# A two-group encoder layer on one core: the second unit's PSUM copies and sum moved ahead of row squares and of the third unit's weights, and the token tiles' transposes moved three steps on

## The chip, the core and the metric

The kernel runs on one core of a Trainium2 chip. A core has engines that run side by side, each with a queue of its own that it works through strictly in order: TensorE (PE in the profile; its weight loads are PEld), VectorE (DVE), ScalarE (ACT), GpSimd (POOL) and SyncE (SP, here used to issue DMAs). An instruction at the head of a queue that waits for another engine holds up all that is queued behind it. Matmuls write into the eight banks of PSUM, and ACT or DVE has to read a bank before other data may be written into it. The metric is the device time of one execution in microseconds; it was 1259.35 us in the median of three runs of the kernel before (1260.97, 1259.35, 1259.35).

## The reference, cut to what matters

One encoder layer is applied to 1024 tokens of a prompt and 256 of a sample, 1280 tokens of 1024 features, with the same weights:

```
h = rms_norm(x, norms[0])
b, c, v = split(h @ conv_w_in, 3)          # 1024 -> 3 x 1024
u = c * v
conv = sum(up[:, j:j + S] * conv_w[j] for j in range(3))
x = x + rms_norm((b * conv) @ conv_w_out, norms[1])
h = rms_norm(x, norms[2])
gate, up = split(h @ ffn_w_in, 2)          # 1024 -> 2 x 2816
x = x + rms_norm((silu(gate) * up) @ ffn_w_out, norms[3])
```

All is float32.

## The kernel before, in words

A float32 product is computed as three matmuls: each operand is split into a high part (a rounded copy, made by ACT) and a low part (what is left, by a DVE subtraction), and high x high, high x low and low x high are added in PSUM. `split`, line 92, does both steps; `make` (line 186) does it for weights, `hi_lo` and `parts` for activations.

The products with the 1024 prompt tokens go by a scheme of seven products of half-size blocks instead of eight. It needs sums and differences of blocks of the activations (the tiles s1 to s4) and of the weights (`make(u, "sums")`, then the pairs t13 and t24). One such product is 12 matmuls of 128x128 by 512 columns (line 213). The sample's 256 tokens are multiplied plainly. A `Block` (line 219) holds one unit, that is, the 128 output features of each of two weight tiles; its products go into the banks x, y and z, and an `Ev` class reads them: `read11`, `read12`, `copy22` and `read21` are ACT copies or DVE products out of bank x between two products that go on accumulating in it, `add11`, `add12` and `add22` are DVE sums that take in bank y or z.

The program has these stages: the first three units of the convolution, called c, v and b (`start`, line 527), the other nine units (loop at line 785), the product with conv_w_out with two norms and transposes back to feature order, by token tiles (loop at line 923), the first FFN product (`ffn_in`), and the second (from line 1553).

Two parts set the order of the work in different ways. `start` and the entry into the FFN stand inside `tc.manual_schedule()`: there each engine's queue has exactly the written order. The loops at lines 785 and 923 stand outside: there a scheduler orders the instructions when the kernel is built, from its own estimate of times, and it may also place instructions of the automatic part between those of `start` that are still to come.

**In `start`, lines 675 to 708.** The second unit (v) has its weights uv, the third (b) ub. TensorE's order is: the product with t24 and s2 into bank x (line 684, below "x6"), t13 with s1 into z (line 689, "z5"), t13 with s3 on top of x (line 690, "x7"), eight small matmuls that spread the norms of the first token chunk over the partitions (`spread(0, 5)`, line 694), t24 with a22 on top of x (line 702, "x4"), and the weights u with s4 on top of z (line 707, "z4"). Then the third unit begins (line 712). x7 may not start before `read12` (line 685) has copied bank x, x4 not before `copy22` (line 692), z4 not before `add22` (line 697) has taken in bank z, and z4 also needs both parts of s4. On ACT, rows of x are squared and summed for the first norm (`next_row`, line 660, which then issues the DMA of a later row from SP's queue into the place that is freed). `norm_of` (line 493) turns the sums into factors with a DVE operation and a power on POOL, and `parts_of_norm` (line 500) makes rq and the high and low parts rh and rl, which `spread` needs.

**In the loop at line 923.** Ten token tiles, in the order 0, 4, 1, 5, 2, 6, 3, 7, then 8 and 9 in the FFN's entry. A tile's product `mm2` (line 847) has eight steps k of six matmuls. After it comes a chain: squares on ACT, factor on DVE and POOL, norm and residual on DVE, squares again, factor again, and the tile ht (line 889). Its eight transposes on TensorE (line 817) are put inside the product of the tile after next, behind `early` of its steps; two copies, one each by ACT and DVE, take them out of PSUM, and `early_sums` (line 910) forms sums from them. The loop's index n counts tiles in this order.

Of the kernel before, what the change touches and what calls it, by code (L numbers as in the profile page):

```python
# [16 lines left out]
KD = D // P  # L17
# [19 lines left out]
def encoder_kernel(ctx: ExitStack, tc: tile.TileContext, xT, x, g0T, gB, cwT, w1, w2, w3, w4, out_p, out_s):  # L37
# [20 lines left out]
    def get(name, shape, dt=F32, kind="b"):  # L58
        if kind == "as":
            kind = "s" if free["s"] else "a"  # L60
        tag = free[kind].pop(0)
        t = mem.tile([P, *shape], dt, tag=tag, name=name)
        held[id(t)] = (t, tag)
        return t

    def put(*tiles):
        for t in tiles:
            tag = held.pop(id(t))[1]
            free[tag[0]].append(tag)
# [19 lines left out]
    def f32(ap):  # L89
        return ap.bitcast(F32)  # L90

    def split(hi, lo, src):
        nc.scalar.activation(hi, src, AF.Copy)
        nc.vector.tensor_tensor(out=lo, in0=src, in1=f32(hi), op=ALU.subtract)

    def sub(out, a, b):
        nc.vector.tensor_tensor(out=out, in0=a, in1=b, op=ALU.subtract)  # L97

    def add(out, a, b):
        return nc.vector.tensor_tensor(out=out, in0=a, in1=b, op=ALU.add)  # L100

    def mul(out, a, b):
        nc.vector.tensor_tensor(out=out, in0=a, in1=b, op=ALU.mult)

    def copy(out, a):
        nc.scalar.activation(out, a, AF.Copy)  # L106
# [3 lines left out]
    def new_ps(name, bank=None):  # L110

        if bank is None:
            bank = turn[0] % 8
            turn[0] += 1
        return ps.tile([P, 512], F32, tag=f"bank{bank}", name=name)
# [9 lines left out]
    def small(n, name, dt=F32):  # L125
        return tmp.tile([P, 4], dt, tag="small", name=name, bufs=8)[:, :n]
# [41 lines left out]
    def uname(u):  # L168
        return "".join(map(str, u))
# [16 lines left out]
    def make(u, what):  # L186

        if u is None:
            return
        rw = raw[u]  # L190
        if what == "sums":
            sub(rw[:, 0], rw[:, 1], rw[:, 0])
            sub(rw[:, 1], rw[:, 2], rw[:, 1])
            sub(rw[:, 2], rw[:, 0], rw[:, 2])
            add(rw[:, 3], rw[:, 3], rw[:, 2])
            return
        blocks = {"g": slice(0, 4, 3), "u": slice(1, 3), "t13": slice(0, 2), "t24": slice(2, 4)}[what]
        t = wb[what, u] = get(f"w{what}{uname(u)}_", [2, 2, 512], F32R)
        split(t[:, 0], t[:, 1], rw[:, blocks])
        sums_made[u] = sums_made.get(u, 0) + what.startswith("t")  # L200
        if sums_made[u] == 2:
            put(raw.pop(u))
# [279 lines left out]
    def load_row(i):  # L482
        sq_rows[i] = get(f"rows{i}", [D], kind="a")
        nc.sync.dma_start(sq_rows[i], x[i])

    def square_row(i):
        t = sq_rows.pop(i)
        nc.scalar.activation(t, t, AF.Square, accum_out=rt[:, i : i + 1])
        put(t)
# [10 lines left out]
    def parts_of_norm(c):  # L500
        t0, n = CH[c]
        i0, m = t0 // P, n // P
        rc = rt[:, i0 : i0 + m]
        mul(rq[:, i0 : i0 + m], rc, rc)
        norms[c] = [small(m, f"r{p}{c}", F32R) for p in "hl"]
        split(*norms[c], rc)

    def spread(c, bank):

        n = CH[c][1]  # L510
        bc = new_ps(f"bc{c}", bank)
        for i in range(n // P):
            for j in range(2):
                nc.tensor.matmul(
                    bc[:, i * P : (i + 1) * P], norms[c][j][:, i : i + 1].to_broadcast([P, P]), ident_r,
                    start=j == 0, stop=j == 1,
                )
        if c < 2:
            nc.scalar.activation(prompt(r2, c), bc, AF.Square)
        else:  # L520
            nc.scalar.activation(samp(r2), by_halves(bc), AF.Square)

    def new_c(name):
        cb[name] = [get(f"{name}{p}", [KH, 512], F32R) for p in "hl"]
        return cb[name]

    def start():
# [85 lines left out]
        def scaled_add(out, src, f0, other, op=ALU.add):  # L613
            for k in range(KH):
                nc.vector.scalar_tensor_tensor(
                    out=out[:, k], in0=src[:, k], scalar=g0k(f0 + k), in1=other[:, k], op0=ALU.mult, op1=op
                )

        def parts(name, src):
            hi, lo = new_c(name)  # L620
            for k in (0, 2):
                copy(hi[:, k : k + 2], src[:, k : k + 2])
            for k in (0, 2):
                sub(lo[:, k : k + 2], src[:, k : k + 2], f32(hi[:, k : k + 2]))


        s1, s2, s3, s4 = (xq[q] for q in ("a21", "a11", "a22", "a12"))
# [14 lines left out]
        ev = EvMul(2, 0)  # L642
        b = Block(uv, ev, banks={q: new_ps(f"{q}v_", n) for q, n in (("x", 0), ("y", 1), ("sg", 2), ("su", 3), ("z", 4))})
# [16 lines left out]
        def next_row(i):  # L660
            square_row(i)
            if i + 2 < NT:
                load_row(i + 2)
# [12 lines left out]
        high3(0)  # L676
        high3(2)
        low3()
        next_row(4)
        parts_of_norm(0)  # L680
        scaled_add(s4, xq["a12"], KH, s2)
        put(s2, s3)
        next_row(5)
        b.run("x", "t24", 0, "s2", False)
        ev.read12(b.bank["x"])
        ev.add11(b.bank["y"], mult=False)
        parts("s4", s4)
        put(s4)
        b.run("z", "t13", 0, "s1", True)
        b.run("x", "t13", 1, "s3", False)  # L690
        b.drop("t13")
        ev.copy22(b.bank["x"])
        make(ub, "g")
        spread(0, 5)
        make(ub, "u")
        make(ub, "sums")
        ev.add22(b.bank["z"])
        next_row(6)
        next_row(7)
        load(SEQ[3])  # L700
# [57 lines left out]
    with tc.manual_schedule():  # L758
        start()
# [25 lines left out]
    for n in range(3, len(SEQ)):  # L785
# [3 lines left out]
        ev = EvC(u[2]) if u[1] == 1 else EvMul(u[1], u[2])  # L789
# [3 lines left out]
        b = Block(u, ev, *follow[:2], final)  # L793
# [23 lines left out]
    def transposes(i, banks=(None, None)):  # L817
        for q in range(2):
            o = new_ps(f"tr{i}_{q}", banks[q])
            for k in range(4):  # L820
                nc.tensor.transpose(
                    o[:, k * P : (k + 1) * P], hts[i][:, (4 * q + k) * P : (4 * q + k + 1) * P], ident
                )
            ov = o.rearrange("p (k t) -> p k t", k=4)
            if i < 8:
                t0 = i % 4 * P
                dst = ar[q, i // 4][:, :, t0 : t0 + P]
                if q:
                    nc.vector.tensor_copy(dst, ov)
                else:  # L830
                    copy(dst, ov)
            else:
                t0 = (i - 8) * P
                copy(hs[0][:, 4 * q : 4 * q + 4, t0 : t0 + P], ov)
                left.append((i, q, ov))
        put(hts.pop(i))
# [10 lines left out]
    def mm2(*tiles, ks=range(KD)):  # L847
        for i in tiles:
            if i not in mx:
                mx[i] = [new_ps(f"mx{i}_{h}", MX_BANKS.get((i, h))) for h in range(2)]  # L850
        for k in ks:
            for i in tiles:
                for j, (w, part) in enumerate(TERMS):
                    for h in range(2):
                        nc.tensor.matmul(  # L855
                            mx[i][h], zs[i][:, part, k], w2t[k][:, w, h * H : (h + 1) * H],
                            start=k == 0 and j == 0, stop=k == KD - 1 and j == 2,
                        )
# [51 lines left out]
    def early_sums(t):  # L910

        a, b, d = (q[:, :, t] for q in (a11, a21, a22))
        split(*(q[:, :, t] for q in cb["a11"]), a)
        add(b, b, d)
        sub(a, a, b)
        add(s3[:, :, t], d, a)
# [6 lines left out]
    for n, i in enumerate(ORDER2[:8]):  # L923
        if n == 0:
            mm2(i, ORDER2[1])
        elif n > 1:
            early = KD - 2 if n < 4 else 1
            mm2(i, ks=range(early))
            transposes(ORDER2[n - 2])
            mm2(i, ks=range(early, KD))  # L930
            if n == 4:
                cb["a11"] = [get(f"a11{p}", [KH, 512], F32R) for p in "hl"]
                s3 = get("s3", [KH, 512])
                early_sums(slice(0, P))
            if n == 6:
                early_sums(slice(P, 2 * P))
        after_mm2(i)
        if n:
            load_z(ORDER2[n + 1])
            load_xt(ORDER2[n + 1])  # L940
        if n == 4:
            load(F0)
            for what in ("g", "u", "sums"):
                make(F0, what)
        if n == 6:
            for what in ("t24", "t13"):
                make(F0, what)
# [691 lines left out]
```

## Time and profile before

| | |
|---|---|
| median of three runs | 1259.35 us |
| the profiled execution, its own time | 1260.64 us |
| its span in the profile | 1258.8 us |
| granted TensorE clock, mean | 0.995 of full speed |
| TensorE busy | 1239.4 us, 98% of the span |
| DVE busy | 834.9 us, 66% |
| ACT busy | 464.2 us, 37% |
| POOL busy | 26.1 us, 2% |

The table is read from the first part of the profile's page and from the run's record. A row of the timeline gives the start and the duration of an instruction (or of a merged run of equal ones, with xcount), its engine, line and operation, what it writes and reads, and in brackets how long the engine had been idle before it and what ended that. Matmuls are pipelined: a row shows 0.39 us for a matmul where the next one starts 0.23 us later. In tile names v and b stand for the second and third unit: xv and zv are banks x and z of the second, xb and zb of the third, wrp__152 are the third unit's raw weights and wrp__611 the fourth's.

### The profile page before, as it was taken

To read this page: it belongs to the slowest core of one execution; us is meant where nothing else is said; L and a number is where in the kernel's file an instruction comes from. 1 tells how busy PE (TensorE), PEld (TensorE's weight loads), DVE (VectorE), ACT (ScalarE), POOL (GpSimd) and SP (SyncE) were. 2 spreads that over 40 slices of the span, in tenths; PEclk is the share of its full clock that TensorE was granted. 3 is DMA by queue.
4 is the path that set the end of the run, shared out by engine and by line. 5 is a ranking of instruction groups with operands and counts; after the bars stand their busy time and mean duration, and the time that the engine had idled before them with its cause. 6 is when DMAs were issued, how large, how long until landed. Compare 5 with 4: busy or idle time off the path is not lost.

```text
span 1258.8 us, 15941 instructions
## 1 busy us (share of the span) xinstructions
PE 1239.4 (98%) x6239; PEld 1053.5 (84%) x6239; DVE 834.9 (66%) x1157; ACT 464.2 (37%) x695; POOL 26.1 (2%) x49
## 2 busy tenths in 40 slices
PE   9899999999999999999999999999999999999997
PEld 7788888888878888888888888888888888888886
DVE  6967855747276697466565764765657479869566
ACT  8633333325143464343343442433434342112011
POOL 0000000000011000000000000000000000000000
PEclk9999999999999999999999999999999999999999
DMA  8313132225954215253453542533526888866894
GB/s 304 110 55 117 68 117 67 81 88 183 318 179 156 101 35 176 92 192 99 136 159 98 171 142 80 184 124 111 192 77 196 282 303 300 272 218 211 287 332 177
DMA packets 186123, 207.37 MB, mean 165 GB/s; under 512 B 8000, under 2 KB 146368, under 8 KB 185024
## 3 DMA queue, kind: packets, MB, share of 16 engines
q1 hardware_dynamic: 185616, 205.83, 48.9%
q8 instruction: 49, 0.80, 0.3%
q10 hardware_dynamic: 432, 0.53, 0.1%
q14 instruction: 26, 0.21, 0.1%
HBM read 134.89 MB, written 71.43 MB: 164 GB/s over the span
## 4 chain that ended last, share of the span: by engine, by line
PE 87%; DVE 5%; DMA 4%; ACT 2%; issue 1%; POOL 1%; SPq 0%; POOLq 0%; DVEq 0%; ACTq 0%
PE xo L1438 12%; PE zo L1438 6%; PE mx L855 5%; PE yo L1438 3%; DMA wrf__3033<-w 1%; PE xf__7466 L213 1%; PE xp__1068 L213 1%; PE xb__651 L213 1%; PE xf__3503 L213 1%; PE xf__4931 L213 1%; PE xf__7645 L213 1%; PE xf__7253 L213 1%; PE xf__7079 L213 1%; PE xf__6866 L213 1%; PE xf__6692 L213 1%
## 5 line engine op out<-in xcount | busy, mean ns | idle before, releaser
L855 PE MATMUL mx<-w2s,zs 128*128 128x512 f32 x480 | 111.1, 391 | 0.0
L855 PEld LDWEIGHTS mx<-w2s,zs 128*128 128x128 f32 x480 | 89.5, 188 | 18.2
L106 ACT ACTIVATE st<-act 128x640 fp32r<-128x640 f32 x77 | 56.8, 737 | 93.6 <-DMA actd<-st 62.7
L97 DVE TENSOR_TENSOR st<-act,st 128x640 fp32r<-128x640 f32 x77 | 63.2, 821 | 21.3 <-ACT st L106 20.8
L100 DVE TENSOR_TENSOR y<-y,xo 128x512 f32<-128x512 f32 x85 | 58.3, 685 | 27.4 <-PE xo L1438 27.1
L1438 PE MATMUL xo<-w4t,us 128*128 128x512 f32 x273 | 68.9, 389 | 0.0
L1438 PEld LDWEIGHTS xo<-w4t,us 128*128 128x128 f32 x273 | 51.3, 188 | 10.6
L1438 PE MATMUL xo<-w4t,ut 128*128 128x512 f32 x222 | 55.5, 389 | 0.0
L106 ACT ACTIVATE w4t<-w4r 128x1024 fp32r<-128x1024 f32 (+1 forms) x23 | 23.5, 1023 | 72.8 <-DVE w4r L97 59.7
L1438 PEld LDWEIGHTS xo<-w4t,ut 128*128 128x128 f32 x222 | 41.7, 188 | 8.7
L100 DVE TENSOR_TENSOR y<-y,zo 128x512 f32<-128x512 f32 x45 | 30.8, 685 | 17.3 <-PE zo L1438 16.9
L1438 PE MATMUL xo<-w4b,ut 128*128 128x512 f32 x165 | 41.6, 390 | 0.0
L1438 PE MATMUL zo<-w4t,ut 128*128 128x512 f32 x165 | 41.5, 389 | 0.0
L1438 PE MATMUL zo<-w4b,ut 128*128 128x512 f32 x165 | 41.5, 389 | 0.0
L1470 ACT ACTIVATE junk<-y 128x1024 f32<-128x1024 f32 (+1 forms) x12 | 11.0, 919 | 73.7 <-DVE y L100 72.3
L1438 PEld LDWEIGHTS xo<-w4b,ut 128*128 128x128 f32 x165 | 31.0, 188 | 6.6
L1438 PEld LDWEIGHTS zo<-w4t,ut 128*128 128x128 f32 x165 | 31.0, 188 | 6.5
L1438 PEld LDWEIGHTS zo<-w4b,ut 128*128 128x128 f32 x165 | 31.0, 188 | 6.4
L430 DVE SCALAR_TENSOR_TENSOR row<-u,cw,row 128x1024 f32<-128x1024 f32 (+1 forms) x32 | 27.7, 880 | 3.7 <-ACT row L428 3.5
L1438 PE MATMUL yo<-w4b,us 128*128 128x512 f32 x114 | 28.9, 389 | 0.0
L106 ACT ACTIVATE w4b<-w4r 128x512 fp32r<-128x512 f32 (+1 forms) x22 | 18.1, 838 | 28.9 <-PE zo L1438 12.5
L97 DVE TENSOR_TENSOR w4t<-w4r,w4t 128x1024 fp32r<-128x1024 f32 (+1 forms) x23 | 26.9, 1174 | 0.8 <-ACT w4t L106 0.8
(2115 smaller groups left out, 3350.9 us busy)
## 6 DMA issues: line engine op xcount, KB each, us to landing
actd<-st SPq DMA_DIRECT2D x154, 320.0 KB, 2.8
ut<-actd SPq DMA_DIRECT2D x20, 1024.0 KB, 6.3
us<-actd SPq DMA_DIRECT2D x62, 256.0 KB, 5.1
ut<-actd SPq DMA_DIRECT2D x16, 768.0 KB, 7.9
zd<-zst SPq DMA_DIRECT2D x32, 320.0 KB, 3.0
zs<-zd SPq DMA_DIRECT2D x8, 1024.0 KB, 6.6
w4r<-w SPq DMA_DIRECT2D x11, 512.0 KB, 4.3
w4r<-w SPq DMA_DIRECT2D x22, 256.0 KB, 5.0
```

Source lines behind the costliest of these rows:

```text
L97: nc.vector.tensor_tensor(out=out, in0=a, in1=b, op=ALU.subtract)
L100: return nc.vector.tensor_tensor(out=out, in0=a, in1=b, op=ALU.add)
L106: nc.scalar.activation(out, a, AF.Copy)
L213: nc.tensor.matmul(out[:, :n], stat(w, k), mov(part, k), start=first and k == 0 and j == 0, stop=last and k == KH - 1 and j == 2, skip_gro ...
L430: nc.vector.scalar_tensor_tensor(out=out, in0=src, scalar=cw[:, j, dd : dd + 1], in1=out, op0=ALU.mult, op1=ALU.add)
L855: nc.tensor.matmul(mx[i][h], zs[i][:, part, k], w2t[k][:, w, h * H : (h + 1) * H], start=k == 0 and j == 0, stop=k == KD - 1 and j == 2,)
L1438: nc.tensor.matmul(acc, stat[n, c, j][:, ap], w[wp], start=starts and jn == 0 and m == 0, stop=jn == len(grp) - 1 and m == 2, skip_group_c ...
L1470: nc.scalar.activation(junk, src, AF.Square, accum_out=acc[:, col : col + 1])
```

## The change

In `start`, `read12` is written ahead of the squares of rows 4 and 5, so that ACT copies bank x first. The scaled sum s4 on DVE is written ahead of `parts_of_norm(0)`. The splitting of s4 is taken apart: the first high half stays ahead of `copy22`, the second goes behind it, and the low halves (DVE) come after that. `add22` is written ahead of the third unit's weights (`make(ub, "g")`, `"u"` and `"sums"`) instead of behind them. TensorE's own order is the same. In the loop over token tiles, the transposes of the tile two back stand behind four steps of the product instead of one, for n = 4 to 7; for n = 2 and 3 they stay behind six.

```
@@ -676,25 +676,28 @@
         high3(0)
         high3(2)
         low3()
+        b.run("x", "t24", 0, "s2", False)
+        ev.read12(b.bank["x"])
         next_row(4)
-        parts_of_norm(0)
+        next_row(5)
         scaled_add(s4, xq["a12"], KH, s2)
         put(s2, s3)
-        next_row(5)
-        b.run("x", "t24", 0, "s2", False)
-        ev.read12(b.bank["x"])
+        parts_of_norm(0)
         ev.add11(b.bank["y"], mult=False)
-        parts("s4", s4)
-        put(s4)
+        high4, low4 = hi_lo("s4", s4)
+        high4(0)
         b.run("z", "t13", 0, "s1", True)
         b.run("x", "t13", 1, "s3", False)
         b.drop("t13")
         ev.copy22(b.bank["x"])
+        high4(2)
+        low4()
+        put(s4)
+        ev.add22(b.bank["z"])
         make(ub, "g")
         spread(0, 5)
         make(ub, "u")
         make(ub, "sums")
-        ev.add22(b.bank["z"])
         next_row(6)
         next_row(7)
         load(SEQ[3])
@@ -924,7 +927,7 @@
         if n == 0:
             mm2(i, ORDER2[1])
         elif n > 1:
-            early = KD - 2 if n < 4 else 1
+            early = KD - 2 if n < 4 else 4
             mm2(i, ks=range(early))
             transposes(ORDER2[n - 2])
             mm2(i, ks=range(early, KD))
```

More of the change, by code (lines that the diff above doesn't have):

```diff
@@ L678, in start @@
         low3()
+        b.run("x", "t24", 0, "s2", False)
+        ev.read12(b.bank["x"])
         next_row(4)
-        parts_of_norm(0)
+        next_row(5)
         scaled_add(s4, xq["a12"], KH, s2)
         put(s2, s3)
-        next_row(5)
-        b.run("x", "t24", 0, "s2", False)
-        ev.read12(b.bank["x"])
+        parts_of_norm(0)
         ev.add11(b.bank["y"], mult=False)
-        parts("s4", s4)
-        put(s4)
+        high4, low4 = hi_lo("s4", s4)
+        high4(0)
         b.run("z", "t13", 0, "s1", True)
@@ L692, in start @@
         ev.copy22(b.bank["x"])
+        high4(2)
+        low4()
+        put(s4)
+        ev.add22(b.bank["z"])
         make(ub, "g")
@@ L696, in start @@
         make(ub, "sums")
-        ev.add22(b.bank["z"])
         next_row(6)
@@ L926, in encoder_kernel @@
         elif n > 1:
-            early = KD - 2 if n < 4 else 1
+            early = KD - 2 if n < 4 else 4
             mm2(i, ks=range(early))
```

## The prediction

> **What bounds the kernel now.** I read the busy shares, then TensorE's waits, then the windows around the longest of them, then the timelines of all engines there.
>
> ```profile
> PE 1239.4 (98%) x6239; PEld 1053.5 (84%) x6239; DVE 834.9 (66%) x1157; ACT 464.2 (37%) x695; POOL 26.1 (2%) x49
> ```
>
> TensorE is the bound. An edit that adds and removes no work, as this one, can only gain what TensorE still loses, so its waits come next (engine, tile, releaser; us in total, times, longest).
>
> ```profile
> PE zv__413 L213 <- DVE c__582 L100: 4.0, 1, 4.0
> PE xv__409 L213 <- ACT c__549 L106: 2.0, 1, 2.0
> PE tr L821 <- DVE n_4t L141: 1.5, 1, 1.5
> ```
>
> Behind the first 10 us hardly more than a fourth wait of 0.7, quoted below, is to be added. The first two lie in the second unit: z4 waited for add22, x7 for read12. The windows show what the longer one also did to the clock (columns: busy time of each engine, granted clock, DMA):
>
> ```profile
> 51.00:54.00 3.00, 1.04 (x5) 0.63 (x4) 2.42 (x6) 2.46 (x5) 0.47 (x1) 1.00 0.73 191
> 60.00:64.00 4.00, 0.00 (x0) 0.00 (x0) 3.90 (x7) 2.00 (x5) 0.00 (x0) 0.80 0.50 186
> 64.00:69.30 5.30, 5.29 (x13) 4.18 (x14) 2.63 (x5) 1.60 (x3) 1.02 (x1) 0.51 0.70 255
> 110.00:330.00 220.00, 219.86 (x1150) 189.53 (x1149) 142.27 (x200) 76.47 (x97) 0.00 (x0) 1.00 0.35 113
> ```
>
> After 2 us of idleness the clock stayed at 1.00; after 4 us it was 0.51 for the whole of z4. From 110 to 330 us TensorE idles 0.14 us, so what is gained ahead of that is not waited away again there.
>
> ```profile
> 50.94 0.39 PE L213 MATMUL zv__413<-s1h,wt13p__455 128*128 128x512 f32 x1
> 53.28 0.50 PE L213 MATMUL xv__409<-s3h,wt13p__455 128*128 128x512 f32 x1 [1.96 <-ACT c__549 L106]
> 56.14 0.22 PE L514 MATMUL bc<-ident_r,rh 128*128 128x128 f32 x1
> 56.99 0.50 PE L213 MATMUL xv__409<-a22h,wt24p__442 128*128 128x512 f32 x1
> 64.01 0.80 PE L213 MATMUL zv__413<-s4h,wup__386 128*128 128x512 f32 x1 [4.02 <-DVE c__582 L100]
> 69.26 0.40 PE L213 MATMUL xb__651<-a11h,wgp__584 128*128 128x512 f32 x1
> 78.34 0.22 PE L514 MATMUL bc<-ident_r,rh 128*128 128x128 f32 x1
> 369.64 11.15 PE L855 MATMUL mx<-w2s,zs 128*128 128x512 f32 x48
> ```
>
> The last row gives the pitch at full clock: 11.15 / 48 = 0.23 us, so twelve matmuls take 2.75. z4 took 69.26 - 64.01 = 5.25, 2.5 more. The one wait thus costs 4.0 + 2.5 us.
>
> **The change, part by part.** The rows of the other engines that it touches:
>
> ```profile
> 48.98 1.06 ACT L488 ACTIVATE rows<-rows 128x1024 f32<-128x1024 f32 x1 [0.74 <-DMA rows<-x]
> 54.59 1.06 ACT L106 ACTIVATE s4h<-xa 128x1024 fp32r<-128x1024 f32 x1 [0.26 <-DVE xa L615]
> 56.34 0.60 ACT L106 ACTIVATE c__582<-xv__409 128x512 f32<-128x512 f32 x1 [0.69 <-PE xv__409 L213]
> 48.23 2.35 DVE L97 TENSOR_TENSOR s3l<-xa,s3h 128x1024 fp32r<-128x1024 f32 x2
> 51.51 0.17 DVE L103 TENSOR_TENSOR rq<-rt 128x4 f32<-128x4 f32 x1 [0.92 <-POOL rt L123]
> 51.82 2.73 DVE L615 SCALAR_TENSOR_TENSOR xa<-xa,g,xa 128x512 f32<-128x512 f32 x4
> 55.07 2.35 DVE L97 TENSOR_TENSOR s4l<-xa,s4h 128x1024 fp32r<-128x1024 f32 x2
> 57.92 1.23 DVE L94 TENSOR_TENSOR wgp__584<-wrp__152,wgp__584 128x1024 fp32r<-128x1024 f32 x1 [0.49 <-ACT wgp__584 L93]
> 63.27 0.68 DVE L100 TENSOR_TENSOR c__582<-c__582,zv__413 128x512 f32<-128x512 f32 x1
> ```
>
> *read12 ahead of two squares.* x6 ends by 48.6 (z5's twelve matmuls start 2.5 us before the last at 50.94). read12, a copy like copy22 (0.60), then runs from about 48.65 to 49.25 and holds up behind it rows 4 and 5's squares, which could not begin before 48.98 for their DMA: they move by about 0.15 us, and so do the row loads that SP issues behind them. x7 starts right behind z5, at 50.94 + 0.23 = 51.17, and ends its issue at 53.9. The 1.96 us go, with the slow first matmul.
>
> *The scaled sum ahead of the norm's parts.* DVE waited 0.92 us for POOL; now s4's sum covers that. DVE comes free at 50.5; the sum and add11 take 55.07 - 51.82 = 3.25, the norm's two small operations about 0.15: the first low half starts at 53.9 and ends at 55.1. The norm's low part is there by 53.4, ahead of the spread at 53.9.
>
> *copy22 between the halves of s4.* High4(0) needs half of the sum (51.9) and ends at 53.0, ahead of x7's last bank write at 54.1. ACT idles until then, and high4(2) and the third unit's weights are queued behind. copy22: 54.1 to 54.7. The spread ends at 53.9 + 0.85 = 54.8 (56.14 to 56.99 in the rows), so x4 starts at 54.8, as before just covered, and ends issue at 57.5. high4(2) 54.6 to 55.65, no later than it ended before.
>
> *add22 ahead of the third unit's weights.* Low4's second half 55.7 to 56.9, add22 (0.68) to 57.5: z4 starts at 57.5 with no wait to speak of. With the clock kept, it ends at 60.3, where b3's x begins: 69.26 - 60.3 = 9.0 us earlier. Each 0.1 us that high4(2) is late costs 0.1.
>
> *What is late next.* DVE and ACT behind add22 gain far less:
>
> ```profile
> 63.39 1.06 ACT L93 ACTIVATE wt24p__628<-wrp__152 128x1024 fp32r<-128x1024 f32 x1 [2.00 <-DVE wrp__152 L100]
> 72.20 0.60 ACT L106 ACTIVATE c__665<-xb__651 128x512 f32<-128x512 f32 x1 [5.88 <-PE xb__651 L213]
> 74.77 1.04 ACT L93 ACTIVATE wgp__671<-wrp__611 128x1024 fp32r<-128x1024 f32 x1
> 77.66 0.15 DVE L94 TENSOR_TENSOR rl<-rt,rh 128x2 fp32r<-128x2 f32 x1
> 62.44 0.59 SPq L184 DMA_DIRECT2D wrp__611<-w  x1
> DMA to landing us min/median/max: 5.9/6.2/6.5
> 64.11 1.02 POOL L123 TENSOR_TENSOR rt<-rt,nhalf 128x4 f32<-128x4 f32 x1 [12.64 <-DVE rt L122]
> ```
>
> From the g weights' low part to add22 was 63.27 - 57.92 = 5.35; starting now at 57.45, the sums end at 62.8, only 0.5 earlier. The norm's scale on DVE, POOL's power (1.02, to 64.0) and on ACT the norm's high part (0.1 to the next start) and t13's high part (about 1.0, of the size of the row at 63.39) follow: ACT is free for c__665 at 65.1. Its 5.88 us of slack are used up: xb is ready at 63.2. From that row to the end of rl took 77.81 - 72.20 = 5.6, bound by ACT's squares of rows 8 and 9 and the fourth unit's weights; so rl of the last chunk is there at 70.7. TensorE, 2.75 per product and 0.85 for a spread, is at the last spread by 60.3 + 3 x 2.75 + 0.85 = 69.4. It waits 1.35 us there, a new wait, too short for the clock by the 51 to 54 window. The spread starts at 70.75 instead of 78.34: 7.6 us gained. The fourth unit's raw weights must land by 67.7 (74.77 - 72.20 after 65.1). Their second load would land by 62.44 + 6.5 less the 1.2 us by which ACT reaches the row squares earlier (copy22 with its wait of 0.69 no longer lies behind high4(2)): 67.7, just in time. All that follows hangs on this spread, on TensorE, DVE, ACT and SP alike, and moves with it.
>
> *The transposes.*
>
> ```profile
> 368.82 1.07 PE L821 MATMUL tr<-ident,ht 128*128 128x128 f32 x8 [0.68 <-DVE ht L892]
> 411.51 1.28 DVE L892 SCALAR_TENSOR_TENSOR ht<-x,n_3t,gb 128x1024 f32<-128x1024 f32 x1 [0.66 <-POOL n_3t L123]
> 415.96 1.04 PE L821 MATMUL tr<-ident,ht 128*128 128x128 f32 x8
> ```
>
> Of four moved groups only n = 4 waited, 0.68 us; eighteen matmuls (4.1 us) now lie ahead of it, so this goes. The 1.5 us wait is n = 2's, which keeps its six steps. The price: copies and early sums come 3.4 us later (4.1 - 0.7). Tightest is tile 3: ht ended at 412.8, TensorE wanted it at 415.96. If tile 6's copy and sums stand ahead of its chain on DVE, it is about 2 us later, still in time. Cost 0.
>
> Sum: 7.6 + 0.7 = 8.3 us. The profiled execution took 1260.64 us, 1.84 over its span of 1258.8 and 1.3 over the median of the runs, 1259.35; a span of 1250.5 follows, and for the median I forecast **1251.0**. Without the new wait it would be 9.0 + 0.7, 1249.7.
>
> **One unknown: POOL's power beside DVE.**
>
> ```profile
> 48.41 3.06 POOL L123 TENSOR_TENSOR rt<-rt,nhalf 128x4 f32<-128x4 f32 x1 [47.10 <-DVE rt L122]
> 452.61 1.45 POOL L123 TENSOR_TENSOR n_9t<-n_9t,nhalf 128x1 f32<-128x1 f32 x1 [7.17 <-DVE n_9t L122]
> 452.45 2.35 DVE L97 TENSOR_TENSOR a22l<-ar,a22h 128x1024 fp32r<-128x1024 f32 x2
> ```
>
> The first power took 3.06 us, the second 1.02, and it ended 0.89 after DVE's pair of subtractions (50.58). After the change DVE goes straight on with s4's sum. The later pair shows a power that ended at 454.06, while DVE's second subtraction ran until 454.8: it got in between two DVE instructions. So the lower bound is no delay (51.47 as before), the upper bound that it waits for DVE to go idle at 53.2, ending at 54.1. I take the lower, by the 452.61 row. [...]
>
> **The rivals.** *The power is held to 54.1:* the norm's high part, high4(0), copy22 and low4 follow one another from there, and x4 and z4 start 1.1 us later; 1252.1. For it the 3.06 us, against it the later pair. Chance 0.12.
>
> *The scheduler's part gives some back:* the loops from line 785 on are ordered at the build by estimated times, which the new front shifts; one more wait as large as those seen (1.5 to 4 us, the clock included) leaves 1252.5 to 1255. For it: the 1.5 us at tile 0 comes from such an order. Against: 0.14 us idle in 220. Chance 0.13.
>
> *Slower, by z4 of the third unit.*
>
> ```profile
> 92.73 0.39 PE L213 MATMUL xp__901<-a11h,wgp__671 128*128 128x512 f32 x1
> 101.11 0.50 PE L213 MATMUL zb__738<-s4h,wup__597 128*128 128x512 f32 x1
> ```
>
> Written order has this product (line 749) right behind x4, at 92.73, but its bank's sum is late; the scheduler put 8.4 us of the fourth unit between. Should the new estimates leave it at its written place, TensorE would idle about 8.4 us and run it at half clock (2.5): 10.9 lost against 8.3, 1262.0. It decides from about 6 us of unfilled wait on (6 + 2.5 against 8.3). Nothing in the change touches these lines. Chance 0.05.
>
> *It does not do what it says:* a product finds another releaser, so that read12, copy22 or add22 were not the last it waited for (s4's parts for z4); the same 4 us and half clock would stay, and 2 to 3 us be gained at best, or nothing: 1256.5 to 1259.4. Against: both rows name the releaser, and s4's low part ended at 57.4, long before 64. Chance 0.07.
>
> **How the numbers follow.** The forecast case (1249.7 to 1252) has 0.63; the first two rivals also gain. About 0.2% (2.5 us) is what a measurement can tell from no change. Faster: 0.63 + 0.12 + 0.13 and a third of the last, 0.90; within: 0.05; slower 0.05. The range holds the forecast case, the power and the greater part of the scheduler's: 1249.0 to 1254.5, its lower end 0.7 under the case without a new wait for the spread of runs.
>
> **What would show it.** Right: x7 behind z5 without idleness, z4 starting near 57.5 with the clock at 1.00, b3's x near 60.3, a wait of about 1.3 us ahead of the last spread near 70.75, ACT's 5.88 us wait at c__665 gone, no wait at n = 4. Wrong: z4 still waiting 3 us or more or at half clock, a power longer than 4 us, or a new wait over 1.5 us after 90 us.

## The result, and the profile after

The changed kernel took 1250.71 us in the median of six runs (1249.41 to 1254.64), the kernel before 1259.99 in six runs beside them (1259.35 to 1262.47). The ratio is 0.9926 with a 95% interval from 0.9910 to 0.9942: 9.3 us less, between 7.3 and 11.3. Forecast were 1251.0 and 8.3 us less. The span of the profiled execution went from 1258.8 to 1248.7 us.

TensorE's waits after the change (engine, tile, releaser; us in total, times, longest), to be set beside those of before; left out are the 1.5 us of the warm-up, the same in both, and two waits of 0.6 and 0.2 us:

```profile
PE tr L824 <- DVE n_4t L141: 0.8, 1, 0.8
PE sgf__3797 L213 <- DVE hsl L97: 0.8, 1, 0.8
PE bc L514 <- DVE rl L94: 0.8, 1, 0.8
```

Both waits of the second unit are gone, and so is the one for ht at n = 4. One is new: bc, the last spread, for rl. The wait at n = 2 (n_4t) is 0.8 instead of 1.5; that of sgf was there before, with the same 0.8 us, and the prediction's count of waits passed over it. TensorE's timeline of the changed kernel:

```profile
53.75 0.22 PE L514 MATMUL bc<-ident_r,rh 128*128 128x128 f32 x1
54.60 0.50 PE L213 MATMUL xv__409<-a22h,wt24p__442 128*128 128x512 f32 x1
57.44 0.47 PE L213 MATMUL zv__413<-s4h,wup__386 128*128 128x512 f32 x1
60.26 0.39 PE L213 MATMUL xb__651<-a11h,wgp__585 128*128 128x512 f32 x1
69.32 0.22 PE L514 MATMUL bc<-ident_r,rh 128*128 128x128 f32 x1
70.32 0.33 PE L514 MATMUL bc<-ident_r,rl 128*128 128x128 f32 x1 [0.79 <-DVE rl L94]
70.71 0.45 PE L213 MATMUL zb__738<-s1h,wt13p__636 128*128 128x512 f32 x1
84.72 0.39 PE L213 MATMUL xp__901<-a11h,wgp__671 128*128 128x512 f32 x1
93.10 0.50 PE L213 MATMUL zb__738<-s4h,wup__598 128*128 128x512 f32 x1
```

The spread starts at 53.75, x4 at 54.60, z4 at 57.44, the third unit's x at 60.26 (69.26 before). z4 takes 60.26 - 57.44 = 2.8 us instead of 5.25, so the clock is kept. The spread's first small matmul, which needs rh alone, starts at 69.32; the next one, which needs rl, a full microsecond later. The third unit's z5 behind it starts at 70.71; it stood 0.40 behind the spread's start of 78.34 before, at 78.74. By there 8.0 us are gained, and the rest moves along: 84.72 to 93.10 is 8.4 us, as 92.73 to 101.11 was.

The other engines of the changed kernel, in the order ACT, DVE, POOL:

```profile
53.95 0.60 ACT L106 ACTIVATE c__579<-xv__409 128x512 f32<-128x512 f32 x1 [1.23 <-PE xv__409 L213]
54.45 1.05 ACT L106 ACTIVATE s4h<-xa 128x1024 fp32r<-128x1024 f32 x1
64.67 0.58 ACT L106 ACTIVATE c__665<-xb__651 128x512 f32<-128x512 f32 x1
47.94 2.35 DVE L97 TENSOR_TENSOR s3l<-xa,s3h 128x1024 fp32r<-128x1024 f32 x2
50.21 2.73 DVE L615 SCALAR_TENSOR_TENSOR xa<-xa,g,xa 128x512 f32<-128x512 f32 x4
55.53 1.23 DVE L97 TENSOR_TENSOR s4l<-xa,s4h 128x1024 fp32r<-128x1024 f32 x1 [0.70 <-ACT s4h L106]
57.27 1.22 DVE L94 TENSOR_TENSOR wgp__585<-wrp__152,wgp__585 128x1024 fp32r<-128x1024 f32 x1
62.32 0.16 DVE L122 TENSOR_SCALAR rt<-rt 128x4 f32<-128x4 f32 x1
70.11 0.15 DVE L94 TENSOR_TENSOR rl<-rt,rh 128x2 fp32r<-128x2 f32 x1
48.12 3.06 POOL L123 TENSOR_TENSOR rt<-rt,nhalf 128x4 f32<-128x4 f32 x1 [46.82 <-DVE rt L122]
```

c__665 has no wait any more: from there ACT and DVE set the pace until rl at 70.11. Two idle pieces are to be seen that the experiments take up: ACT waited 1.23 us for copy22 with half of s4 still to split, and DVE then 0.70 us for that half.

### The profile page after: what moved, and what is told of

The parts are those of the page before. It is cut to its first block, busy times and chain, and to the rows that moved or that the text cites. A ratio compares the mean times of both kernels' runs of the same rounds, so it can differ in the third digit from the quotient of the medians.

```text
span 1248.7 us, 15941 instructions
## 1 busy us (share of the span) xinstructions
PE 1236.0 (99%) x6239; PEld 1052.2 (84%) x6239; DVE 835.0 (67%) x1157; ACT 463.9 (37%) x695; POOL 25.6 (2%) x49
## 4 chain that ended last, share of the span: by engine, by line
PE 91%; DMA 3%; DVE 3%; ACT 2%; issue 1%; SPq 0%; POOL 0%; POOLq 0%; DVEq 0%; ACTq 0%
PE xo L1441 12%; PE mx L858 6%; PE zo L1441 6%; PE yo L1441 3%; DMA wrf__3033<-w 1%; PE xp__1068 L213 1%; PE xf__3503 L213 1%; PE xp__901 L213 1%; PE xf__7645 L213 1%; PE xf__7466 L213 1%; PE xf__7253 L213 1%; PE xf__7079 L213 1%; PE xf__6866 L213 1%; PE xf__6692 L213 1%; PE xf__6479 L213 1%; PE xf__6305 L213 1%
```

## The experiments

The theory (W): the gain is the two waits of the second unit, the half clock behind the longer one and the wait at n = 4, less what comes late next. The rivals: the gain comes from the later part (S), or the half clock has a cause of its own (N).

**The front alone.** In the changed kernel:

```
-            early = KD - 2 if n < 4 else 4
+            early = KD - 2 if n < 4 else 1
```

> The edits in start alone; the transposes stay behind one step. Theory W (the gain is the two waits of the second unit and the half clock behind the longer one): z4 starts near 57.5, the third unit's x near 60.3, the last spread's low part near 70.3, about 8.0 us under the kernel before; the 0.7 us wait for ht at n = 4 comes back. Time about 1251.5 to 1252, 0.7 over the changed kernel. Rival S (most of it comes from the later part, its transposes and the order that the scheduler makes): at most 5 us under the kernel before, 1255 or more.

1251.84 us, ratio to the kernel before 0.9937 [0.9922, 0.9951]. TensorE's timeline of this kernel, at the last spread, the third unit's z5 and n = 4:

```profile
70.16 0.33 PE L514 MATMUL bc<-ident_r,rl 128*128 128x128 f32 x1 [0.78 <-DVE rl L94]
70.55 0.44 PE L213 MATMUL zb__738<-s1h,wt13p__636 128*128 128x512 f32 x1
359.57 1.06 PE L824 MATMUL tr<-ident,ht 128*128 128x128 f32 x8 [0.63 <-DVE ht L895]
```

W holds: the front makes nearly all of it, and the wait at n = 4 is back with 0.63 us.

**The transposes alone.** In the kernel before, the same line changed from 1 to 4.

> The transposes three steps on, alone; start as before. Theory W: the wait at n = 4 goes, nothing else; x7 still waits 2.0 us and z4 4.0 us with the clock at 0.5. 0.5 to 0.8 us under the kernel before, not to be told from it. Rival S: 3 us or more under it. The wait at n = 2, 1.5 us before and 0.8 in the changed kernel, tells whether the transposes moved it: W says that it hangs on when the load of the first FFN weights lands and may be anything between 0.8 and 1.6 here.

1258.97 us, ratio 0.9998 [0.9989, 1.0007]: no difference that can be told. TensorE's waits in it:

```profile
PE zv__413 L213 <- DVE c__582 L100: 3.9, 1, 3.9
PE xv__409 L213 <- ACT c__549 L106: 2.0, 1, 2.0
PE tr L821 <- DVE n_4t L141: 1.7, 1, 1.7
```

S falls. ht is no longer among them, so the 0.7 us are gained; but n = 2 waits 1.7 us here. In the profiles that wait took 1.5 us (before) and 0.7 (front alone) without this edit, and with it 0.8, 1.7, 1.2, 0.5, 0.4 and 0.7 us or was not there at all. ACT had a copy of the first FFN weights ahead of this tile's squares and waited for their load (4.60 us before, 3.92 after, 4.81 here). So the 0.7 us between the two profiles at this place can't be put down to the change.

This run brought something else. Its front is that of the kernel before, and x7 waited 2.03 us as it did there; but there the clock had stayed. Here TensorE's timeline and the windows of 2 us show:

```profile
52.64 0.50 PE L213 MATMUL xv__409<-s3h,wt13p__455 128*128 128x512 f32 x1 [2.03 <-ACT c__549 L106]
56.88 0.31 PE L514 MATMUL bc<-ident_r,rh 128*128 128x128 f32 x1
```

```profile
52.00:54.00 2.00, 1.36 (x6) 1.12 (x7) 2.00 (x4) 1.71 (x5) 0.00 (x0) 0.99 0.48 123
54.00:56.00 2.00, 2.00 (x6) 1.56 (x5) 2.00 (x3) 1.00 (x1) 0.00 (x0) 0.50 0.51 207
56.00:58.00 2.00, 2.00 (x12) 1.79 (x10) 0.78 (x1) 0.88 (x2) 0.00 (x0) 0.66 0.00 0
```

x7 took 56.88 - 52.64 = 4.2 us instead of 2.9: the clock fell to 0.50 behind a wait of 2.03 us, and only at 53.95, when TensorE had been at work again for 1.3 us. z4 came off worse too: it waited 3.89 us, began at 64.79, and the clock was back only at 71.02, in the third unit's x; half of these 6.2 us, 3.1, were lost, against 2.5 in the profile before.

**add22 late.** In the changed kernel:

```
-        ev.add22(b.bank["z"])
         make(ub, "g")
...
         make(ub, "sums")
+        ev.add22(b.bank["z"])
```

> The changed kernel with add22 put back behind the third unit's g, u and sums on DVE. Theory W: add22 ends near 62.4, z4 waits about 5 us and runs at half clock (5.25 us instead of 2.75), so the third unit's x begins near 67.7 instead of 60.3; the 0.8 us wait at the last spread then goes, since DVE and ACT are done by then; 6 to 7 us over the changed kernel, about 1257. Rival N (the clock at z4 has another cause than the wait): z4 waits 5 us but runs at full clock, 4 us over the changed kernel. Rival (another releaser than add22): no change.

1257.18 us, ratio 0.9981 [0.9971, 0.9991]. TensorE's timeline:

```profile
62.01 0.80 PE L213 MATMUL zv__413<-s4h,wup__386 128*128 128x512 f32 x1 [4.97 <-DVE c__579 L100]
66.74 0.40 PE L213 MATMUL xb__651<-a11h,wgp__584 128*128 128x512 f32 x1
76.21 0.45 PE L213 MATMUL zb__738<-s1h,wt13p__636 128*128 128x512 f32 x1
```

The wait is back with 4.97 us, z4 takes 4.7 us, the wait at the last spread is gone, and z5 stands 5.5 us later than in the changed kernel (70.71). So this one line is worth most of the change. The medians by the ratios lie 0.0055 apart, about 7 us. W holds; N's 4 us at full clock is not what is seen.

**read12 late.**

```
-        b.run("x", "t24", 0, "s2", False)
-        ev.read12(b.bank["x"])
         next_row(4)
-        next_row(5)
...
         parts_of_norm(0)
+        next_row(5)
+        b.run("x", "t24", 0, "s2", False)
+        ev.read12(b.bank["x"])
```

> The changed kernel with read12 put back behind row 4's square, the norm's parts and row 5's square on ACT; add22 stays early. Theory W: read12 near 52.4 to 53.0, x7 waits about 2 us, all of copy22, high4(2), low4 and add22 move with it and z4 starts near 59.6 without a wait of its own; ACT's and DVE's later work moves as well, so the last spread moves by about 2.1 us: 2.0 to 2.3 us over the changed kernel, 1252.9. Rival: the slack found at the last spread (0.8 us wait) takes part of it, 1.2 to 1.4 us over.

```profile
53.05 0.50 PE L213 MATMUL xv__409<-s3h,wt13p__455 128*128 128x512 f32 x1 [2.38 <-ACT c__549 L106]
```

In the profile x7 waited 2.38 us, the third unit's x began at 62.46 and z5 at 72.90: 2.2 us later than in the changed kernel, as W has it, and the new wait at the last spread stayed at 0.77 us, so no slack took part of it. The time, though, was 1254.43 us, ratio 0.9958 [0.9942, 0.9974], about 4 us over the changed kernel's and not 2.2, though the two intervals touch. The profiled execution kept its clock (1.00 in every window of 2 us from 48 to 70) behind the 2.38 us; if others did not, as the transposes' run did not, that is another 1.4 us or so. The two slowest of the four executions (1256.24 and 1255.29) had a mean granted clock of 0.997, the other two 0.998, which points the same way; that this is the difference was not shown.

**add22 in between.** Three kernels with add22 behind g, behind g and u, and behind g, u and two of the four operations of the sums, to make TensorE wait ahead of z4 by 1 to 3.6 us.

> The changed kernel with add22 behind the third unit's g (one subtraction of 1.1 us ahead of it on DVE). Theory W: z4 waits about 1.1 us at full clock; the wait at the last spread shrinks by as much as TensorE is late there, so the time is within 0.5 us of the changed kernel. Rival N: the clock goes with any wait ahead of z4, 2.5 us more.

> add22 behind g and u. z4 waits about 2.2 us. x7's wait of 2.0 us in the kernel before left the clock at 1.00, so theory W has z4 at full clock here too, 1.4 us over the changed kernel. If the clock's limit lies lower than that: z4 in 5.25 us and about 4 us over.

> add22 behind g, u and two of the four operations of the weight sums. z4 waits about 3.6 us. Theory W has no row for a wait between 2.0 (full clock) and 4.0 us (half clock): 2.8 us over the changed kernel if the clock stays, 5.3 if it is halved for z4.

Behind g: 1252.33 us in one execution. z4 waited 0.94 us and took 2.85; z5 began at 70.48, no later than in the changed kernel (70.71), since the wait at the last spread went in exchange. In that profile another 1.2 us at n = 2 and 0.6 at the fifth unit were waited, which the edit does not touch.

Behind g and u (1252.59 us in one execution), and amid the sums (1251.80): z4's first matmul and the third unit's first, one kernel in each fence.

```profile
59.57 0.50 PE L213 MATMUL zv__413<-s4h,wup__386 128*128 128x512 f32 x1 [2.19 <-DVE c__579 L100]
64.01 0.39 PE L213 MATMUL xb__651<-a11h,wgp__584 128*128 128x512 f32 x1
```

```profile
60.63 0.50 PE L213 MATMUL zv__413<-s4h,wup__386 128*128 128x512 f32 x1 [3.52 <-DVE c__579 L100]
63.49 0.39 PE L213 MATMUL xb__651<-a11h,wgp__584 128*128 128x512 f32 x1
```

The shorter wait, 2.19 us, lost the clock (z4 took 4.4 us); the longer one, 3.52, kept it (2.9). No limit on the length of the wait explains that. The same two kernels were run again:

> The same kernel as the one with add22 behind g and u, which waited 2.19 us ahead of z4 and ran part of z4 at half clock, while another waited 3.52 us and kept the clock. Theory P (whether a wait of 2 to 4 us halves the clock hangs on when it falls, and differs from execution to execution of one kernel): the wait is 2.1 to 2.3 us again, and z4 takes anything from 2.85 to 5.3 us; it need not be the 4.44 of the first look. Rival L (a fixed limit; something in this order of instructions makes it lower than in the other): z4 takes 4.4 us again, within 0.2.

> The same kernel as the one with add22 in the midst of the weight sums, which waited 3.52 us and kept the full clock. Theory P: the wait is 3.4 to 3.6 us again, and this time the clock may well be halved; longer waits meet it more often. Rival L: z4 takes 2.86 us again, within 0.2.

```profile
59.51 0.50 PE L213 MATMUL zv__413<-s4h,wup__386 128*128 128x512 f32 x1 [2.18 <-DVE c__579 L100]
62.38 0.39 PE L213 MATMUL xb__651<-a11h,wgp__584 128*128 128x512 f32 x1
```

```profile
60.80 0.79 PE L213 MATMUL zv__413<-s4h,wup__386 128*128 128x512 f32 x1 [3.52 <-DVE c__579 L100]
65.17 0.39 PE L213 MATMUL xb__651<-a11h,wgp__584 128*128 128x512 f32 x1
```

The same waits, 2.18 and 3.52 us, and the outcomes the other way round: 2.9 us for z4 in the first, 4.4 in the second. So the clock behind a wait of this size differs from execution to execution of one kernel; a fixed limit on the length of the wait is refuted. What it hangs on instead is in the last section. The medians of these runs were 1252.99 us (0.9951 [0.9936, 0.9966], six runs from 1251.23 to 1257.49) and 1255.24 us (0.9969 [0.9957, 0.9981]).

**A first power at the start.** In the changed kernel:

```
+    ones = const.tile([P, 1], F32, tag="ones", name="ones")
+    nc.vector.memset(ones, 1.0)
+    nc.gpsimd.tensor_tensor(out=ones, in0=ones, in1=nhalf[:, :1], op=ALU.pow)
```

> The changed kernel with one power on POOL, on a tile of ones, at the very start, that nothing reads. It tells why the first power of the norm takes 3.06 us and the second 1.02. If it is the first use of the operation: 1.0 to 1.9 us now, ending by 50.0, and the row squares' norm waits for it no more; if it is VectorE's two subtractions: 3.06 as before, ending 0.89 us behind them. In both cases no change in time (within 0.5 us of the changed kernel), since ACT needs it by 51.7 only.

1248.73 us in one execution. POOL's timeline:

```profile
1.27 0.56 POOL L75 TENSOR_TENSOR ones<-ones,nhalf 128x1 f32<-128x1 f32 x1
47.86 3.06 POOL L126 TENSOR_TENSOR rt<-rt,nhalf 128x4 f32<-128x4 f32 x1 [46.03 <-DVE rt L125]
```

It is not the first use: the very first power took 0.56 us, and the norm's still 3.06. The time was expected within 0.5 us of the changed kernel's 1250.71 and lay 2.0 under it. In this profile the front started 0.6 us earlier (z4 at 56.82), and the waits of 0.8 us at n = 2 and of 0.6 at xf were absent, against a new one of 0.4 at the fifth unit; one execution does not tell whether the edit has a part in that.

**s4 in one piece.** In the changed kernel:

```
         high4(0)
+        high4(2)
+        low4()
+        put(s4)
         b.run("z", "t13", 0, "s1", True)
...
         ev.copy22(b.bank["x"])
-        high4(2)
-        low4()
-        put(s4)
```

> The changed kernel with s4 split in one piece: both high halves on ACT ahead of copy22, both low halves on DVE ahead of add22. By the changed kernel's rows ACT sat idle 1.23 us ahead of copy22, and s4 was whole at 52.95, so the second high half fits there and ends by 54.0, just when bank x is complete. Theory W: copy22 is at most 0.1 us later, DVE's idle 0.7 us ahead of the second low half goes, ACT's and DVE's later work is 0.7 to 0.9 us earlier and so is the low part for the last spread: the new wait there (0.8 us) goes, 0.7 us under the changed kernel. Rival (the split was needed): copy22 is late by half a copy or more, x4 waits, 0.5 us or more over the changed kernel.

1250.39 us, ratio 0.9931 [0.9919, 0.9944]. ACT's, DVE's and TensorE's timelines of this kernel:

```profile
51.64 2.21 ACT L106 ACTIVATE s4h<-xa 128x1024 fp32r<-128x1024 f32 x2
53.76 0.58 ACT L106 ACTIVATE c__582<-xv__409 128x512 f32<-128x512 f32 x1
69.15 0.15 DVE L94 TENSOR_TENSOR rl<-rt,rh 128x2 fp32r<-128x2 f32 x1
69.74 0.45 PE L213 MATMUL zb__738<-s1h,wt13p__636 128*128 128x512 f32 x1
```

In the profile it does what W says: ACT is done with both high halves just as bank x is complete, copy22 follows without loss, rl is 1.0 us earlier, and of the wait at the last spread only 0.1 us of idle time is left (too short for the list of waits); z5 begins at 69.74 instead of 70.71 (0.2 of that is an earlier start of the whole front). The split of s4 around copy22 was not needed. Against the kernel before, the times of this kernel and of the changed one (0.9926) cannot be told apart.

**And seven steps at n = 2.** As the last kernel, and in the loop:

```
+            early = KD - 1 if n == 2 else KD - 2 if n == 3 else 4
```

> As the kernel with s4 in one piece, and at n = 2 the transposes stand behind seven steps of the product instead of six (1.4 us later). Theory W: the wait there (0.8 to 1.5 us, for a tile that waits for the load of the first FFN weights) goes or nearly so: 0.8 to 1.4 us under the kernel with s4 in one piece, about 1249. Rival: the copies of this tile, later by 1.4 us, are late for the next ones, and nothing is gained.

1248.29 us in five runs (1247.84 to 1248.88), ratio 0.9914 [0.9900, 0.9927]; all five lie below the five of the kernel with s4 in one piece (1249.27 to 1251.79), on the same chip. The transposes at n = 2 start at 341.73 without a wait. The medians differ by 2.1 us, more than the 0.8 to 1.4 expected, and more than the profiles' spans do (1247.5 and 1246.5); what the rest is, stays open. It is the fastest kernel of the study.

## Why the prediction was right, point by point

- *read12 ahead of two squares:* x7 goes on right behind z5; the spread behind it starts at 53.75 (53.9 forecast). The kernel with read12 late puts 2.2 us back in the profile.
- *copy22 between the halves of s4, add22 early:* z4 at 57.44 (57.5 forecast), x at 60.26 (60.3). The kernel with add22 late shows that it was indeed this sum that z4 had waited for.
- *What is late next:* right in kind and place, a little too large. ACT is free for c__665 at 64.67 (65.1 forecast): the weights and sums took 62.32 - 57.27 = 5.05 us instead of 5.35, since waits in the old row spacing were gone. rl then came 5.6 us behind c__665, as forecast (70.26 less 64.67). TensorE lost 1.0 us there instead of 1.35, and 8.0 us were gained by z5 instead of 7.6.
- *The transposes:* 0.63 us, shown by the front alone; 0.7 forecast. No copy or sum came late.
- *POOL's power:* it took 3.06 us again and ended 0.89 behind the pair of subtractions (51.18 against 47.94 + 2.35 = 50.29), although DVE went straight on with s4's sum. The lower bound was the right one, and the rival falls. That the pair of subtractions held the power until about 50.29 is an estimate from these ends. Why the border between the two subtractions then did not let it in, and the one in the 452.61 row did (1.45 us, ended at 454.06 while the pair ran until 454.8), the runs do not show. s4's sum was not held up by the 0.9 us of power beside it: its four operations took 2.73 us, as they did before with no power beside them.
- *The other rivals:* the third unit's late product kept its 8.4 us of other work ahead, and no wait above 1 us appeared behind 90 us.
- *The step that failed:* that a wait of 1.35 us is "too short for the clock", by the one window of 51 to 54 us. The wait did no harm, but the reason was one execution of a thing that varies: 2.03 us lost the clock with the front of the kernel before, 2.18 us did once and did not once, 3.52 likewise. The kernel before may therefore have lost up to 1.4 us at x7 as well, in some executions, and z4's half clock, 2.5 us in the sum, varies too: 3.1 in the transposes' run. How much of the 9.3 us against 8.3 these two make was not measured. The shortest wait that lost it in these runs was 2.03 us; waits of 0.8 to 0.94 us kept it in each profile.

## What to carry to other kernels

When a bound engine waits twice in a row for copies and sums of its own banks, put those at the head of the reading engines' queues, and then follow these engines on by their row spacing: the new limit stands where their work, not shifted by as much, meets the bound engine again. Look in the profile after for idle time of the reading engines around the moved instructions; it showed at once that one of the edits, the split of s4, was not needed. And count a wait of TensorE of the size that lost the clock here (2.03 us was the shortest, and x7 took about 1.4 us longer behind it) with the clock that it may cost, from several executions, not from the one that was profiled.

## What the runs showed of the hardware that was not expected

In these profiles the half clock behind a wait came in stretches of 3.4 us, or of twice that. From the windows of 2 us, with the granted clock c in each, the time at half clock is the sum of 2 x (1 - c) x 2 us. c is the third column from the end; the windows on either side have 1.00. First the kernel with add22 behind g and u, in its first profile, then the kernel before:

```profile
60.00:62.00 2.00, 2.00 (x7) 1.62 (x6) 1.90 (x4) 0.00 (x0) 0.00 (x0) 0.59 0.76 291
62.00:64.00 2.00, 2.00 (x6) 1.52 (x5) 0.90 (x3) 1.55 (x3) 1.02 (x1) 0.56 0.93 360
```

```profile
62.00:64.00 2.00, 0.00 (x0) 0.00 (x0) 1.97 (x4) 0.61 (x1) 0.00 (x0) 0.60 0.90 348
64.00:66.00 2.00, 1.99 (x5) 1.61 (x6) 1.41 (x4) 1.28 (x3) 1.02 (x1) 0.50 0.88 286
66.00:68.00 2.00, 2.00 (x6) 1.54 (x5) 1.22 (x1) 0.32 (x1) 0.00 (x0) 0.50 0.92 368
68.00:70.00 2.00, 2.00 (x8) 1.59 (x7) 0.00 (x0) 0.00 (x0) 0.00 (x0) 0.70 0.06 23
```

The first gives (0.41 + 0.44) x 4 = 3.4 us, the second (0.40 + 0.50 + 0.50 + 0.30) x 4 = 6.8. The transposes' run at x7 gives (0.01 + 0.50 + 0.34) x 4 = 3.4. In the first kernel the clock fell at about 60.36 (62 - 0.41 x 4), 0.8 us after TensorE was back at work (59.57).

Within each profile in which the clock fell behind a wait, all its changes lie on one grid of 3.4 us. The transposes' run shows it best; from 66 to 70 us and from 1256 on its windows have 0.50:

```profile
64.00:66.00 2.00, 1.21 (x3) 1.02 (x4) 1.55 (x4) 1.11 (x2) 1.02 (x1) 0.55 1.01 406
70.00:72.00 2.00, 2.00 (x8) 1.54 (x7) 0.00 (x0) 0.00 (x0) 0.00 (x0) 0.75 0.00 0
1254.00:1256.00 2.00, 0.00 (x0) 0.00 (x0) 1.41 (x2) 0.00 (x0) 0.25 (x1) 0.86 0.74 276
```

With windows of 0.1 us, the clock fell at 53.95, rose at 57.36, fell at 64.19, rose at 71.02, and fell behind TensorE's last work at 1255.44. The distances are 1, 2, 2 and 347 times 3.413 us. The four other profiles in which it fell twice have the same step: from fall to rise it was 6.83 us in the kernel before (62.38 to 69.21, and 1191.25 us, 349 times 3.413, from that fall to the last at 1253.63), and by the windows of 2 us 6.8 with add22 late (59.24 to 66.08), 3.4 behind g and u (60.36 to 63.76) and 3.4 amid the sums, again (60.68 to 64.08). The grid lies differently in each execution: the first border behind 50 us is at 50.54 in the transposes' run and at 52.14, 52.41, 53.53 and 53.85 in these four. Where the clock was kept at the waits (read12 late; behind g and u, again; amid the sums), the borders are an estimate, counted back from the last fall by this step. Split at the borders, the waits of over 1 us in the second unit come out so:

| kernel, product | wait, us | of it in each stretch of the grid, us | clock |
|---|---|---|---|
| before, x7 | 1.96 | 0.82, 1.14 | kept |
| read12 late, x7 | 2.38 | 1.03, 1.35 | kept |
| behind g and u, again, z4 | 2.18 | 0.60, 1.58 | kept |
| amid the sums, z4 | 3.52 | 1.74, 1.78 | kept |
| transposes alone, x7 | 2.03 | 2.03 | lost |
| behind g and u, z4 | 2.19 | 2.19 | lost |
| add22 late, z4 | 4.97 | 2.21, 2.76 | lost |
| before, z4 | 4.02 | 2.39, 1.63 | lost |
| transposes alone, z4 | 3.89 | 3.29, 0.60 | lost |
| amid the sums, again, z4 | 3.52 | 3.39, 0.13 | lost |

At the end of each stretch that held 2.03 us or more of a wait the clock fell (or, for the second one of add22 late, stayed down); at the end of none that held 1.78 or less did it fall. In these ten waits the clock thus went by the idle time within a stretch and not by the length of the wait; where between 1.78 and 2.03 us it turns, these runs do not show. It came back at the end of the first stretch with at most 0.13 us of waiting (with 0.60 it did not yet). A wait of 1.96 to 4.97 us thus cost its own length here, and with it nothing or about 1.4 to 3.1 us, depending on how it fell into these stretches.
